# Queueing modulations behind the short convolution, casts of summed weights behind operand splits, and gate loads behind adding DMAs

## The chip, the core and the metric

The kernel runs on one core of one Trainium2 chip. The metric is device time in microseconds (us) for one launch. In the text PE is TensorE, DVE is VectorE, ACT is ScalarE, POOL is GpSimd and SP is SyncE; PEld is the load of stationary weights into PE. "L857" is line 857 of the kernel before. Every engine works through its own queue in order: an instruction that waits holds up all that stand behind it on the same engine.

## The reference

One layer of a hybrid encoder over 1024 tokens of 1024 channels, in fp32:

```
mod = silu(c) @ w_ada + b_ada                 # six vectors of 1024
h   = rms_norm(x) * (1 + sc1) + sh1
b_s, c_s, v_s, v_c, gl_c, gates = split(h @ w_in)      # w_in: 1024 x 7168
y_a = (b_s * causal_conv3(c_s * v_s)) @ w_short_out
u   = silu(layer_norm(causal_conv31(v_c * sigmoid(gl_c)) + bias))
y_b = u @ w_conf_out
x  += g1 * ((sigmoid(gate_a) * y_a + sigmoid(gate_b) * y_b) @ w_o)
h2  = rms_norm(x) * (1 + sc2) + sh2
x  += g2 * ((silu(h2 @ w_a) * (h2 @ w_b)) @ w_ffn_out)
out = rms_norm(x)
```

The vector `mod` depends on `c` alone, so its pieces can be computed at any time before they are used; g1, sc2, sh2 and g2 are wanted only after the projections and the mixers.

## The kernel before

**Matmuls.** All channels lie on partitions (128 at a time) and the 1024 tokens along the free axis, in two halves of 512. To keep fp32 accuracy each operand is split into a high part (a rounding cast, on ACT) and a low part (operand minus high part, on DVE or POOL); for weights that is `wh` (L243) and `wl` (L244). Each tile product is then three matmuls, high x high (L504), high x low (L505) and low x high (L507).

**Products and duals.** A matrix product is taken in 2 x 2 blocks with seven block products instead of eight; they are named "1265734" in the order in which they run. Products "5", "6", "7" and "3" need sums of weight blocks and of operand blocks. A *dual* is a pair of row blocks of the output that go through the seven products together. The input projection has 14 duals; duals 3 to 9 make the pairs u (conformer input), p (c_s * v_s) and q (b_s), duals 10 to 13 the gates. Results build up in PSUM banks "x", "y" and "z", and DVE and ACT read them out after each product (L866, L869, L873, L922). W_short_out (the "ya" stage), W_conf_out ("yb"), W_o and the two FFN matrices follow. In yb the two duals 0 and 1 are interleaved by `CONF_ORDER`: (0,"1") (1,"1") (0,"2") (1,"2") (0,"5") (1,"5") (0,"6") (1,"6") (0,"3") (0,"7") (1,"7") (0,"4") (1,"4") (1,"3").

**Weights.** They are fetched and split two products ahead. SP loads raw blocks (L227). In duals 3 to 9 POOL adds blocks and makes `wl`. In yb the sums are made in two ways: product "6" adds on DVE (L407), while "5", "7" and "3" use an adding DMA on POOL's queue (L397), which adds the second block to the raw tile that holds the first.

**Work between the products.** The depthwise convolution over 31 taps runs on DVE (L1158), one tap per instruction, spread over the input projection. The short convolution of a finished p row (`short_conv`: two ACT instructions at L854, then four DVE instructions at L857) uses the dual's two "x" banks as scratch; PE may write these banks again only when L857 is through. The pieces of `mod` are dot products of a 128 x 1024 block of w_ada with silu(c), one DVE instruction each (`modulation_of`, L485). Fourteen of these are spread over duals 3 to 9, two in each, at products "3" and "5" (`MOD_AT`). The block is loaded into the raw buffer that `dual_units.home` names, and the L485 is queued behind the product's last matmul.

**Order.** The program is traced once, and a scheduler at build time orders each engine's queue; `tc.issue_after(ins)` makes what is traced inside it stand behind `ins` in its queue. It adds no wait of its own. The order that comes out is static.

**Yb's side work.** The operands of each product are split as z..h (ACT, L544) and z..l (DVE, L545), the operands of "6" after a sum on DVE (t2z, L557). The results are multiplied by the gates: `gates_b` loads gate tiles `gb` on POOL's queue (L1421), DVE multiplies, and an adding DMA on POOL's queue (L1394) adds the product to the merged tile `ma`.

Of the kernel before, what the change touches and what calls it, by code (L numbers as in the profile page):

```python
# [38 lines left out]
ALU = mybir.AluOpType  # L39
# [28 lines left out]
BEGUN = 2  # L68
# [33 lines left out]
GATED = 10  # L102
# [17 lines left out]
CONF_ORDER = [(d, m) for m in "1256" for d in range(2)] + [(0, "3")] + [(d, m) for m in "74" for d in range(2)] + [(1, "3")]  # L120


MOD_FROM, MOD_AT = 16, "53"

# [12 lines left out]
def block_kernel(ctx: ExitStack, tc: tile.TileContext, x0, xT, c, vecs, ada, w_first, w_plain, w_duals,  # L139
                 w_short, w_conf, w_o, w_fi, w_fo0, w_fo1, outT):  # L140
    nc = tc.nc

    def pool(name, bufs, **kw):
        return ctx.enter_context(tc.tile_pool(name=name, bufs=bufs, **kw))
# [13 lines left out]
    rawp = pool("raw", 3)  # L158
# [8 lines left out]
    rawbp = pool("raw_b", 2, side="right")  # L167
# [7 lines left out]
    def hl_tile(name, dt=F32R):  # L175
        return tp.tile([P, H], dt, tag="t", name=name)
# [7 lines left out]
    def f32(t):  # L184
        return t.bitcast(F32)

    halves = (slice(0, H), slice(H, T))
# [21 lines left out]
    def col(base, k):  # L209
        return vec[:, base + k : base + k + 1]  # L210

    def modc(i):
        return mod[:, i : i + 1]
# [4 lines left out]
    def raw_tile(n=1024, home=None):  # L218

        if home is None:  # L220
            raws.append(raws.pop(0))
        return (home or raws[-1]).tile([P, 1024], F32, tag="raw", name="raw")[:, :n]

    def load(src, n=1024, home=None):
        raw = raw_tile(n, home)
        with tc.issue_after(x1_load[0]) if x1_load else ExitStack():
            load.ins = nc.sync.dma_start(raw, src).ins  # L227
        return raw
# [8 lines left out]
    def split_w(raw, n, after=(), lo_engine=nc.vector):  # L237
        wh = whp.tile([P, 1024], F32R, tag="wh", name="wh")[:, :n]
        wl = wlp.tile([P, 1024], F32R, tag="wl", name="wl")[:, :n]
        with ExitStack() as order:  # L240
            for ins in after:
                order.enter_context(tc.issue_after(ins))
            hi = nc.scalar.copy(wh, raw)  # L243
            lo = lo_engine.tensor_tensor(wl, raw, f32(wh), ALU.subtract)  # L244
        split_w.hi, split_w.lo = hi.ins, lo.ins
        if n == T and lo_engine is nc.gpsimd:
            pool_los.append((hi.ins, lo.ins))
        return wh, wl
# [130 lines left out]

        return {m: (lambda m=m: unit(m)) for m in PRODUCTS}  # L380

    conf_homes = [rawp, rawbp, rawp]

    def conf_units(mats, d):


        a = {}
        mat = dict(zip(("11", "12", "21", "22"), mats))

        def get(b, home=None):  # L390
            if home is None:
                conf_homes.append(conf_homes.pop(0))
                home = conf_homes[-1]
            return load(mat[b], home=home)

        def add(raw, b):
            nc.gpsimd.dma_start(raw, mat[b], accum_op=ALU.add)  # L397
            return raw

        def unit(m):  # L400
            if m == "5":
                raw = a["s1"] = add(get("22"), "21")
            elif m == "6":
                lo = split_w.lo
                raw = a["s2"] = get("11", (rawp, rawbp)[d])
                with tc.issue_after(lo):
                    nc.vector.tensor_tensor(raw, raw, a["s1"], ALU.add)  # L407
            elif m == "7":
                raw = add(get("21"), "11")
            elif m == "3":  # L410
                raw = add(a["s2"], "12")
            else:
                raw = get({"1": "11", "2": "12", "4": "22"}[m])
            return split_w(raw, 1024)

        return {m: (lambda m=m: unit(m)) for m in PRODUCTS}

    def gated_units(mats):
# [46 lines left out]
    def next_w(ahead=AHEAD):  # L465

        fetch(ahead + 1)
        return ready.pop(0)
# [14 lines left out]
    def modulation_of(i, raw):  # L483
        b = ADA_ORDER[i]
        nc.vector.tensor_tensor_reduce(  # L485
            out=raw, in0=raw, in1=cs, scale=1.0, scalar=col(V_ADA, b),
            op0=ALU.mult, op1=ALU.add, accum_out=modc(b),
        )
# [27 lines left out]
    def product(banks, m, t, evac=None, between=None, y_tile=ps2_tile, z_tile=ps_tile, onto="", by_k=False):  # L516


        w = next_w()
        b = {"1": "x", "6": "x", "7": "x", "4": "x", "2": "y", "5": "z", "3": "z"}[m]  # L520
        n = len(t)
        if by_k:
            for k in range(n):
                for p in range(2):
                    c0 = (p * n + k) * P
                    mm3([banks[b, p]], slice(c0, c0 + P), w, [t[k]], m not in onto and k == 0, k == n - 1, m in onto)
            for p in range(2):
                evac(p, m, banks[b, p])
            return
        for p in range(2):  # L530
            if (b, p) not in banks:
                banks[b, p] = {"x": ps_tile, "y": y_tile, "z": z_tile}[b](b)
            ps = banks[b, p]
            for k in range(n):
                c0 = (p * n + k) * P
                mm3([ps], slice(c0, c0 + P), w, [t[k]], m in "125" and m not in onto and k == 0, k == n - 1, m in "6734" + onto)
            if evac:
                evac(p, m, ps)
            if between and p == 0:
                between()  # L540
# [158 lines left out]
    gate_dram = {(b, j): dram.tile([P, T], F32, name=f"gate_{b}{j}") for b in "ab" for j in range(KC)}  # L699

    def uc_tile(name, n=T + CK - 1, dt=F32):
        return ucp.tile([P, T + CK - 1], dt, tag="uc", name=name)[:, :n]
# [147 lines left out]
    def short_conv(j, p, banks):  # L850

        sc[j] = uc_tile(f"sc{j}", T)
        for h, ps in enumerate(banks):
            nc.scalar.activation(ps, p[:, h * H : (h + 1) * H], AF.Copy, scale=col(V_SW, j))  # L854
        for h, ps in enumerate(banks):
            for s in range(1, SK):
                nc.vector.scalar_tensor_tensor(  # L857
                    out=ps if s < SK - 1 else sc[j][:, halves[h]], in0=p[:, h * H + s : (h + 1) * H + s],
                    scalar=col(V_SW + s * KC, j), in1=ps, op0=ALU.mult, op1=ALU.add,
                )  # L860


    reads = []
# [200 lines left out]
    def more_operands():  # L1064

        for p in range(2):
            nc.scalar.copy(win_banks[0]["x", p], m1[p])
        sums = t_split.ins
        for m, i, h in (("5", 0, 0), ("7", 0, 1), ("4", KH, 0)):
            for k in range(KH):  # L1070
                if m == "7" and k:
                    with tc.issue_after(sums):
                        nc.vector.tensor_tensor(x[k, 1], x[k + KH, 1], x[k, 1], ALU.subtract)
                th[m][k] = t_pair("t")
                t_split(x[k + i, h], *th[m][k])
        reads.append((0.0, t_split.ins))
# [4 lines left out]
    b = {}  # L1081
# [152 lines left out]
    n_mod = 0  # L1234
    for d, m in win_order:
        if (d, m) == (n_duals - 2, PRODUCTS[-2]):
            q_steps.pop(0)()
        if d + 1 >= GATED and d + 1 < n_duals:
            if m == PRODUCTS[-3]:
                win_evacs[d + 1].begin()  # L1240
            elif m == PRODUCTS[-1]:
                for p in range(2):
                    win_evacs[d + 1].bring(p)
        if d + 1 < BEGUN and m == PRODUCTS[-1]:
            for p in range(2):
                nc.scalar.copy(win_banks[d + 1]["x", p], m1[2 * (d + 1) + p])
        mod_raw = load(ada[MOD_FROM + n_mod], home=dual_units.home) if m in MOD_AT and BEGUN < d < GATED else None
        with tc.issue_after(mm3.ins) if (d, m) == (0, "6") else ExitStack():
            product(win_banks[d], m, th[m], win_evacs[d], onto="2")
        if (d, m) == win_order[0]:  # L1250
            more_operands()
            begin_gated("2", next_w(), streams[3:], 1)
        if (d, m) == (0, PRODUCTS[-1]):
            for h in range(2):
                tot.append(hl_tile(f"tot{h}", dt=F32))
                nc.gpsimd.memset(tot[h], 0.0)
        if win_order.index((d, m)) >= len(win_order) - 7:
            q_steps.pop(0)()
        if mod_raw is not None:
            with tc.issue_after(mm3.ins):  # L1260
                modulation_of(MOD_FROM + n_mod, mod_raw)
            n_mod += 1
    while late:
        late.pop(0)()
# [149 lines left out]
    gbs = {}  # L1414

    def gates_b(d, m):
        row, h = {"2": (0, 0), "7": (1, 1), "3": (0, 1), "4": (1, 0)}.get(m, (0, None))
        for i in range(2 * (h is not None)):
            j = 4 * d + 2 * i + row
            gbs[j, h] = g_tile("gb")  # L1420
            nc.gpsimd.dma_start(gbs[j, h], gate_dram["b", j][:, halves[h]])  # L1421

    yb_banks = [{} for _ in range(2)]
    for p in range(2):
# [353 lines left out]
    for g in range(FINAL):  # L1778
        n = 2 * GROUPS[g] * P
# [216 lines left out]
```

## Time and profile before

| what | value |
|---|---|
| median of 3 runs | 1468.63 us (1468.36 to 1471.03) |
| the profiled execution's own time | 1469.08 us |
| its span from the first to the last instruction | 1467.3 us |
| PE busy | 1436.7 us (98%), granted clock 0.99 |
| DVE busy | 1215.4 us (83%) |
| ACT busy | 652.4 us (44%) |
| POOL busy | 522.6 us (36%) |

The profiled execution is 0.45 us above the median, and 1.78 us above its span. A busy PE does not show how fast its clock ran, so the count of matmuls in a stretch of fixed length says more than the busy share. The stages by time: first operands to about 150 us, duals 2 to 13 to about 565, ya to 650, yb to 733, W_o to 790, the FFN to 1440.

### The profile page before, as it was taken

The numbers are of one execution on the slowest core, as the hardware profiler recorded it, in microseconds if no ns is written. First come the engines' busy times: TensorE is split into PE (matmuls) and PEld (weight loads), VectorE is DVE, ScalarE is ACT, GpSimd is POOL, SyncE is SP. The second block draws the span as 40 slices with busy tenths as digits, with TensorE's granted clock in tenths as the row PEclk, the third lists the DMA queues.
The fourth block names the chain that finished last, engine by engine and source line by source line (L and its number), as shares of the span: only waits on it lengthen the run. The fifth ranks groups of instructions, "written<-read, shape, count | busy, mean of one in ns | idle before, by whom it ended". The sixth has DMA issues, their size and how long they took to land.

```text
span 1467.3 us, 17736 instructions
## 1 busy us (share of the span) xinstructions
PE 1436.7 (98%) x6322; PEld 1177.6 (80%) x6322; DVE 1215.4 (83%) x1665; ACT 652.4 (44%) x955; POOL 522.6 (36%) x496
## 2 busy tenths in 40 slices
PE   9999999999989999997999999999999999999997
PEld 4888888777878888886788888888888888888887
DVE  7987999899989999987897799877776666866676
ACT  4873333333333446565535465444444443322235
POOL 0017776776676562012221001110111015663405
PEclk9999999999999999998999999999999999999999
DMA  9743133232335569768694536655554449996903
GB/s 354 274 153 99 59 125 105 101 115 101 125 106 181 165 205 323 218 201 184 165 332 163 172 115 217 218 176 174 173 183 144 150 143 350 390 371 194 356 1 115
DMA packets 95946, 275.04 MB, mean 187 GB/s; under 512 B 10945, under 2 KB 12993, under 8 KB 95858
## 3 DMA queue, kind: packets, MB, share of 16 engines
q1 hardware_dynamic: 46672, 148.92, 30.0%
q0 software_dynamic: 44000, 111.36, 25.1%
q10 hardware_dynamic: 5186, 13.64, 2.4%
q8 instruction: 49, 0.80, 0.2%
q14 instruction: 39, 0.32, 0.1%
HBM read 203.09 MB, written 67.63 MB: 185 GB/s over the span
## 4 chain that ended last, share of the span: by engine, by line
PE 84%; DVE 6%; POOL 4%; issue 2%; DMA 2%; ACT 0%; POOLq 0%; DVEq 0%; ACTq 0%
PE bank L504 10%; PE bank L505 10%; PE bank L507 10%; PE x L507 8%; PE x L505 8%; PE x L504 8%; PE z L507 4%; PE z L505 4%; PE z L504 4%; PE y L505 2%; PE y L504 2%; PE y L507 2%; PE mix L505 2%; PE mix L504 2%; PE mix L507 2%
## 5 line engine op out<-in xcount | busy, mean ns | idle before, releaser
L243 ACT CAST wh<-raw 128x1024 fp32r<-128x1024 f32 (+2 forms) x254 | 262.9, 1037 | 423.9 <-PE bank L505 139.0
L244 DVE TENSOR_TENSOR wl<-raw,wh 128x1024 fp32r<-128x1024 f32 (+2 forms) x176 | 212.4, 1208 | 52.9 <-ACT wh L243 51.1
L244 POOL TENSOR_TENSOR wl<-raw,wh 128x1024 fp32r<-128x1024 f32 x78 | 194.2, 2494 | 112.4 <-ACT wh L243 112.4
L1158 DVE SCALAR_TENSOR_TENSOR c<-diff,vec,c 128x512 f32<-128x512 f32 x232 | 164.3, 746 | 1.0
L1634 POOL DMA_DIRECT2D hid<-stage x70 | 37.4, 535 | 342.6 <-DVE stage L553 322.5
L504 PE MATMUL bank<-th,wh 128*128 128x512 f32 x336 | 132.5, 394 | 10.1 <-DVE sc L857 10.1
L507 PE MATMUL bank<-th,wl 128*128 128x512 f32 x336 | 132.0, 393 | 0.0
L505 PE MATMUL bank<-tl,wh 128*128 128x512 f32 x336 | 131.7, 392 | 0.0
L504 PEld LDWEIGHTS bank<-th,wh 128*128 128x128 f32 x336 | 63.9, 190 | 25.0 <-DVE sc L857 11.7
L505 PEld LDWEIGHTS bank<-tl,wh 128*128 128x128 f32 x336 | 63.9, 190 | 13.3
L507 PEld LDWEIGHTS bank<-th,wl 128*128 128x128 f32 x336 | 63.6, 189 | 13.4
L1158 DVE SCALAR_TENSOR_TENSOR c<-u,wsum,c 128x512 f32<-128x512 f32 x96 | 69.7, 746 | 0.6
L504 PE MATMUL x<-th,wh 128*128 128x512 f32 x176 | 68.5, 389 | 0.0
L505 PE MATMUL x<-tl,wh 128*128 128x512 f32 x176 | 68.5, 389 | 0.0
L507 PE MATMUL x<-th,wl 128*128 128x512 f32 x176 | 68.4, 390 | 0.0
L552 ACT CAST stage<-g 128x512 fp32r<-128x512 f32 x60 | 37.3, 621 | 58.9 <-DMA hid<-stage 37.7
L553 DVE TENSOR_TENSOR stage<-g,stage 128x512 fp32r<-128x512 f32 x60 | 41.2, 688 | 24.8 <-ACT stage L552 24.6
L1658 POOL DMA_DIRECT2D th<-hid x77 | 41.1, 534 | 51.8 <-PE x L507 28.0
L485 DVE CUSTOM_DVE_ANT_0 raw<-raw,cs,vec 128x1024 f32<-128x1024 f32 x24 | 42.7, 1783 | 11.8 <-DMA raw<-in_ada 11.0
L1658 POOL DMA_DIRECT2D tl<-hid x77 | 41.2, 535 | 19.0 <-DMA tl<-hid 3.2
L264 DVE TENSOR_TENSOR raw<-raw 128x1024 f32<-128x1024 f32 (+1 forms) x15 | 17.8, 1187 | 31.4 <-DMA raw<-in_w_fi 19.0
L504 PE MATMUL bank<-t2h,wh 128*128 128x512 f32 x112 | 43.6, 389 | 0.0
(830 smaller groups left out, 4156.6 us busy)
## 6 DMA issues: line engine op xcount, KB each, us to landing
hid<-stage POOLq DMA_DIRECT2D x70, 512.0 KB, 4.5
raw<-in_w_duals SPq DMA_DIRECT2D x65, 512.0 KB, 3.7
raw<-in_w_fi SPq DMA_DIRECT2D x54, 512.0 KB, 4.5
th<-hid POOLq DMA_DIRECT2D x77, 256.0 KB, 5.9
tl<-hid POOLq DMA_DIRECT2D x77, 256.0 KB, 5.9
ada<-in_ada SPq DMA_DIRECT2D x24, 512.0 KB, 5.5
raw<-in_ada SPq DMA_DIRECT2D x24, 512.0 KB, 4.3
raw<-in_w_fo SPq DMA_DIRECT2D x16, 512.0 KB, 6.1
```

Of the source, the lines that this page charges most:

```text
L243: hi = nc.scalar.copy(wh, raw)
L244: lo = lo_engine.tensor_tensor(wl, raw, f32(wh), ALU.subtract)
L264: eng.tensor_tensor(a["s1"], a["21"], a["22"], ALU.add)
L485: nc.vector.tensor_tensor_reduce(out=raw, in0=raw, in1=cs, scale=1.0, scalar=col(V_ADA, b), op0=ALU.mult, op1=ALU.add, accum_out=modc(b),)
L504: nc.tensor.matmul(ps, wh, xh, start=first, stop=False, skip_group_check=again)
L505: nc.tensor.matmul(ps, wh, xl, start=False, stop=False, skip_group_check=again)
L507: mm3.ins = nc.tensor.matmul(ps, wl, xh, start=False, stop=last, skip_group_check=again).ins
L552: t_split.act = nc.scalar.copy(hi, src).ins
L553: t_split.ins = nc.vector.tensor_tensor(lo, src, f32(hi), ALU.subtract).ins
L1158: tap.ins = nc.vector.scalar_tensor_tensor(out=out, in0=src[:, s : s + H], scalar=wt, in1=acc, op0=ALU.mult, op1=ALU.add).ins
L1634: nc.gpsimd.dma_start(hid_dram[key], s)
L1658: nc.gpsimd.dma_start(t, hid_dram[key][:, s])
```

## The change

There are three edits.

```diff
-MOD_FROM, MOD_AT = 16, "53"
+MOD_FROM = 16
...
-    conf_homes = [rawp, rawbp, rawp]
+    conf_homes, conf_adds = [rawp, rawbp, rawp], []
...
         def add(raw, b):
-            nc.gpsimd.dma_start(raw, mat[b], accum_op=ALU.add)
+            conf_adds.append(nc.gpsimd.dma_start(raw, mat[b], accum_op=ALU.add).ins)
             return raw
...
-            return split_w(raw, 1024)
+            return split_w(raw, 1024, () if m in "12" else (split.act, split.ins))
...
-                nc.vector.scalar_tensor_tensor(
+                short_conv.ins = nc.vector.scalar_tensor_tensor(
                     out=ps if s < SK - 1 else sc[j][:, halves[h]], in0=p[:, h * H + s : (h + 1) * H + s],
                     scalar=col(V_SW + s * KC, j), in1=ps, op0=ALU.mult, op1=ALU.add,
-                )
+                ).ins
...
-        mod_raw = load(ada[MOD_FROM + n_mod], home=dual_units.home) if m in MOD_AT and BEGUN < d < GATED else None
...
-        if mod_raw is not None:
-            with tc.issue_after(mm3.ins):
-                modulation_of(MOD_FROM + n_mod, mod_raw)
+        for n in range('55'.count(m) * (BEGUN < d < GATED)):
+            with tc.issue_after(short_conv.ins):
+                modulation_of(MOD_FROM + n_mod, load(ada[MOD_FROM + n_mod], home=(dual_units.home,dual_units.home)[n_mod % 2]))
             n_mod += 1
...
-            nc.gpsimd.dma_start(gbs[j, h], gate_dram["b", j][:, halves[h]])
+            with tc.issue_after(conf_adds[-1]) if conf_adds else ExitStack():
+                nc.gpsimd.dma_start(gbs[j, h], gate_dram["b", j][:, halves[h]])
```

**Edit A** issues both modulations of a dual at product "5" (before: one at "5", one at "3"), loads their blocks after the product instead of before it, and queues both L485 behind the last short-convolution instruction traced so far instead of behind the product's matmuls. On DVE, at dual 8, where two p rows are convolved (sc_3038 and sc_3045; p_2832 is the second row's input), the rows are these before:

```order
L485 ISA raw,mod<-raw,cs,vec 128x1024
L485 ISA mod 128x1
L1158 SCALAR_TENSOR_TENSOR c_4368<-diff,vec,c_4368 128x512 x2
L857 SCALAR_TENSOR_TENSOR bank<-p_2817,vec,bank 128x512 x2
L857 SCALAR_TENSOR_TENSOR sc_3038<-p_2817,vec,bank 128x512 x2
L869 TENSOR_TENSOR sc_3038<-bank,sc_3038 128x512
L857 SCALAR_TENSOR_TENSOR bank<-p_2832,vec,bank 128x512
L485 ISA raw,mod<-raw,cs,vec 128x1024
L485 ISA mod 128x1
L857 SCALAR_TENSOR_TENSOR sc_3045<-p_2832,vec,bank 128x512
```

and in the changed kernel these:

```order
L857 SCALAR_TENSOR_TENSOR bank<-p_2817,vec,bank 128x512 x2
L857 SCALAR_TENSOR_TENSOR sc_3038<-p_2817,vec,bank 128x512 x2
L869 TENSOR_TENSOR sc_3038<-bank,sc_3038 128x512
L857 SCALAR_TENSOR_TENSOR bank<-p_2832,vec,bank 128x512 x2
L857 SCALAR_TENSOR_TENSOR sc_3045<-p_2832,vec,bank 128x512 x2
L706 MEMSET u_3082 128x30
L485 ISA raw,mod<-raw,cs,vec 128x1024
L485 ISA mod 128x1
L485 ISA raw,mod<-raw,cs,vec 128x1024
L485 ISA mod 128x1
```

All eight L857 now stand ahead of both L485. The rows p_1001, p_1834, p_2094 and p_2328 change in the same way, with four L857 each.

**Edit B** queues the cast and the subtraction of every yb weight, except for products "1" and "2", behind the operand split (ACT and DVE) that was traced last. On ACT, around the operands z6 of product "6", the queue before reads

```order
L243 CAST wh<-raw 128x1024
L544 CAST z6h<-t2z 128x512
L1275 ACTIVATE cv_4987<-cv_4987,vec 128x512
L243 CAST wh<-raw 128x1024
L544 CAST z6h<-t2z 128x512
L1401 COPY vz<-y 128x512 x2
L544 CAST z6h<-t2z 128x512 x2
L1401 COPY vz<-bank 128x512 x2
L544 CAST z3h<-cv_4835 128x512
```

and in the changed kernel (whose lines 1274 and 1400 are the old 1275 and 1401)

```order
L544 CAST z6h<-t2z 128x512
L1274 ACTIVATE cv_4987<-cv_4987,vec 128x512
L544 CAST z6h<-t2z 128x512
L243 CAST wh<-raw 128x1024
L1400 COPY vz<-y 128x512 x2
L544 CAST z6h<-t2z 128x512 x2
L243 CAST wh<-raw 128x1024
L1400 COPY vz<-bank 128x512 x2
L544 CAST z3h<-cv_4835 128x512
```

Each of the two casts moves back: the cast for (1,"6"), which stood ahead of the first z6h, stands behind the second, and the cast for (0,"3"), which stood ahead of the second z6h, stands behind the fourth.

**Edit C** queues each gate load behind the last adding DMA of the weights traced so far. On POOL's queue, in the same place, before:

```order
L1394 DMA ma_4731<-gb 128x512
L1394 DMA ma_4745<-gb 128x512
L1421 DMA gb<-gate_b_121 128x512
L1421 DMA gb<-gate_b_123 128x512
L397 DMA raw<-in_w_conf 128x1024 x2
```

and in the changed kernel (L1393 is the old L1394):

```order
L1393 DMA ma_4731<-gb 128x512
L1393 DMA ma_4745<-gb 128x512
L397 DMA raw<-in_w_conf 128x1024 x2
L1421 DMA gb<-gate_b_119 128x512
L1421 DMA gb<-gate_b_121 128x512
```

The two adding DMAs, for (0,"3") and (0,"7"), stand directly behind the adds into `ma`, ahead of the gate loads 119, 121 and 123.

## The prediction

> **What bounds the kernel now.** I read the page first, then what PE waited for, then the stretches in which it waited.
>
> ```profile
> PE 1436.7 (98%) x6322; PEld 1177.6 (80%) x6322; DVE 1215.4 (83%) x1665; ACT 652.4 (44%) x955; POOL 522.6 (36%) x496
> ```
>
> PE is busy 98% of the span, so nothing can be won except where PE stands still or runs at a lowered clock. The list of PE's waits has only two entries of size:
>
> ```profile
> PE bank L504 <- DVE sc L857: 10.1, 4, 4.8
> PE bank L504 <- ACT z6h L544: 8.4, 1, 8.4
> PE clock L720 <- DVE ones_r L738: 1.6, 1, 1.6
> ```
>
> Four waits, 10.1 us together, are for the short convolution, and one of 8.4 us is for an operand split in yb. The third kind lies at the start, where nothing is changed. A wait also costs the matmuls that run slowly after it. For that I count matmuls in stretches of 10 us (columns: PE busy with its count, PEld, DVE, ACT, POOL, PE clock, DMA share, GB/s) against an undisturbed 100 us:
>
> ```profile
> 450.00:550.00 100.00, 100.00 (x443) 82.82 (x442) 97.05 (x128) 43.40 (x64) 62.84 (x30) 1.00 0.62 188
> 270.00:280.00 10.00, 8.26 (x36) 6.50 (x36) 10.00 (x16) 2.69 (x5) 2.82 (x2) 1.00 0.47 160
> 310.00:320.00 10.00, 8.26 (x37) 6.53 (x36) 9.64 (x16) 2.70 (x5) 2.92 (x2) 1.00 0.48 160
> 350.00:360.00 10.00, 8.22 (x29) 6.27 (x29) 9.89 (x17) 2.71 (x4) 3.07 (x2) 0.83 0.46 154
> 430.00:440.00 10.00, 5.21 (x18) 3.94 (x17) 9.92 (x14) 4.68 (x7) 5.48 (x2) 0.85 0.56 195
> 680.00:690.00 10.00, 3.22 (x15) 2.33 (x13) 2.54 (x4) 0.74 (x2) 4.42 (x6) 0.81 0.97 208
> 690.00:700.00 10.00, 8.41 (x27) 6.75 (x28) 8.45 (x13) 3.74 (x6) 0.00 (x0) 0.68 0.63 157
> 700.00:710.00 10.00, 9.76 (x41) 6.89 (x40) 6.23 (x9) 7.48 (x13) 0.00 (x0) 1.00 0.33 106
> ```
>
> 443 matmuls in 100 us are 44.3 in 10 us, or 0.226 us each. The four stretches of the duals lack 8.3, 7.3, 15.3 and 26.3, together 57.2 matmuls or 12.9 us. The three of yb hold 83 of 132.9 and lack 49.9, or 11.3 us. So at most 24.2 us are to be had, and the floor is 1469.08 - 24.2 = 1444.9 us by the profiled execution, 1444.4 by the median, which is 0.45 lower.
>
> **Edit A, what it removes.** At the first of the four waits DVE and ACT do this:
>
> ```profile
> 262.92 1.30 ACT L854 ACTIVATE bank<-p,vec 128x512 f32<-128x512 f32 x2
> 261.77 3.38 DVE L1158 SCALAR_TENSOR_TENSOR c<-diff,vec,c 128x512 f32<-128x512 f32 x5
> 268.92 2.60 DVE L485 CUSTOM_DVE_ANT_0 raw<-raw,cs,vec 128x1024 f32<-128x1024 f32 x1 [3.77 <-DMA raw<-in_ada]
> 272.10 1.40 DVE L857 SCALAR_TENSOR_TENSOR bank<-p,vec,bank 128x512 f32<-128x512 f32 x2
> 273.42 1.40 DVE L857 SCALAR_TENSOR_TENSOR sc<-p,vec,bank 128x512 f32<-128x512 f32 x2
> ```
>
> L857 has its inputs at 264.2, when L854 ends, and DVE is free at 265.15. But the L485 ahead of it waits 3.77 us for its block of w_ada and works 2.60 us, so L857 starts at 272.10, 6.9 us late, and PE (waiting 1.7 us by the stretch 270 to 280) gets its banks. With L485 behind L857, some 5 us of margin take the place of this wait. The largest wait, at the dual with two p rows, is on the chain of waits (start, length):
>
> ```profile
> 422.98 3.57 DMA raw<-in_ada
> 426.71 1.29 DVE raw L485
> 433.35 3.28 DVE raw L485
> 436.64 0.67 DVE sc L857
> 437.36 0.79 PE bank L504
> ```
>
> Both L485 stand ahead of the last L857. Taken out they free DVE from 422.98 to 428.00 and from 433.35 to 436.64, 8.3 us, where PE lacks 26.3 matmuls (5.9 us). PE arrives earlier by what the first three waits free (30.9 matmuls, 7.0 us), so here L857's margin is 8.3 - 5.9 = 2.4 us plus what DVE has caught up by then, less 7.0.
>
> **Whether DVE can follow** is thus the question for A. It sums up as follows:
>
> ```profile
> L485 DVE CUSTOM_DVE_ANT_0 raw<-raw,cs,vec 128x1024 f32<-128x1024 f32 x10 | 21.5, 2155 | 8.9 <-DMA raw<-in_ada 8.9
> L431 DVE TENSOR_TENSOR raw<-raw 128x1024 f32<-128x1024 f32 x2 | 4.1, 2063 | 2.1 <-DMA raw<-in_w_duals 2.0
> L485 DVE CUSTOM_DVE_ANT_0 ada<-ada,cs,vec x24: 1276/1280/1284, 11.8 to 1058.2; 128x1024 f32<-128x1024 f32 x24
> 433.20 2.35 POOL L244 TENSOR_TENSOR wl<-raw,wh 128x1024 fp32r<-128x1024 f32 x1 [7.89 <-ACT wh L243]
> ```
>
> From 270 to 480 DVE idles 8.9 us for w_ada and 2.0 for weights; both can go, since behind L857 the loads have 5 us more. Also, ten L485 take 2155 ns where one alone takes 1280, together 8.75 us: the one at 433.35 ends 1.0 us after POOL's L244 ends. I expect the L485 to meet POOL as often as now and book none of this. DVE then wins 10.9 us by 480 (bounds 8.9 and 8.9 + 2.0 + 8.75 = 19.6) and PE 12.9, so DVE falls 2.0 us further behind PE (bounds 4.0 and none). Seven duals hold their DVE work unchanged. What DVE can be behind shows where it is furthest, at dual 11:
>
> ```profile
> 507.95 0.68 DVE L866 TENSOR_TENSOR sig<-bank,sig 128x512 f32<-128x512 f32 x1
> 509.62 0.39 PE L504 MATMUL bank<-th,wh 128*128 128x512 f32 x1
> ```
>
> The read-out of product "7" ends at 508.63 and PE writes the same bank for "4" at 509.62: 1.0 us to spare. 2.0 - 1.0 = 1.0 us of waiting is left, so **A gives 12.9 - 1.0 = 11.9 us** (bounds 12.9 and 12.9 - 3.0 = 9.9). The margin at the two-p dual is 2.4 + 5.2 (8.9 less the 3.7 from 422.98 to 426.71 counted there already) - 7.0 = 0.6 us, thin but positive.
>
> [...]
>
> **Edits B and C.** The chain of waits through yb:
>
> ```profile
> 674.81 7.18 DMA ma<-gb
> 682.28 0.55 POOL gb L1421
> 682.83 7.04 DMA raw<-in_w_conf
> 689.97 1.04 ACT wh L243
> 691.01 0.53 ACT z6h L544
> 691.59 1.22 PE bank L504 x2
> ```
>
> The second z6h stands on ACT behind the cast for (0,"3"). That cast waits for its adding DMA, which stands on POOL behind gate loads that wait for the buffers of the adds into ma. C issues the adding DMA when its raw tile is free, some 5 us sooner (about 677.8), so it lands near 677.8 + 7.04 = 684.9. B moves the cast behind the fourth z6h, so z6h no longer depends on either. What is late next is DVE, which stood still here:
>
> ```profile
> 677.12 1.22 DVE L407 TENSOR_TENSOR raw<-raw 128x1024 f32<-128x1024 f32 x1
> 679.50 1.23 DVE L244 TENSOR_TENSOR wl<-raw,wh 128x1024 fp32r<-128x1024 f32 x1
> 691.04 1.23 DVE L244 TENSOR_TENSOR wl<-raw,wh 128x1024 fp32r<-128x1024 f32 x1 [8.51 <-ACT wh L243]
> ```
>
> Laid out in the new order from 677.12 with the lengths that these instructions have now (0.60 us from start to start for a 128 x 512 row, 1.14 for L244 and L407), DVE gives z6l of the four operands at 680.7, 683.1, 686.7 and 689.1, with one L244 between the second and the third. PE starts product "6" at 681.2 and interleaves four groups, so it wants the third z6l after 25 matmuls (686.9) and the fourth after 36 (689.4): on time by 0.2. PE then ends "6" at 692.1, and the first z3h, behind the read-out of (0,"6") on ACT, is ready at about 692.5 and z3l at 693.1, so about 1.0 us of waiting stays. **B and C give 11.3 - 1.0 = 10.3 us** (upper bound 11.3; lower bound 6, if DVE comes 4 us later here, the length of the two L407 and L244 ahead of z6, and again 1.0 is left). The adding DMA shares the DMA engines with the gate loads (0.97 busy in 680 to 690); even 4 us later, at 689, it would land as the cast's turn comes.
>
> All that follows yb has no PE wait in the list, so it moves up unchanged, and so does the 1.78 us of the profiled time outside its span. No instruction is added.
>
> **Sum.** 1469.08 - 11.9 - 10.3 = 1446.9 us by the profiled execution, less 0.45: **1446.4 us** for the median.
>
> **Rivals.**
>
> *A's waits only move.* Two L485 in a row each meet a POOL instruction: 2.35 + 1.28 = 3.6 us instead of 2.155, 1.5 us more for each of 14, or 21 us of DVE time; DVE then wins nothing by 480 and PE waits at L866 or L857 for all that A was to free. For it: DVE is 97% busy from 450 to 550. Against: between the pairs POOL idles too (7.89 us ahead of 433.20). Only B and C remain: 1468.63 - 10.3 = 1458.3 us. Half of it gives 1452.
>
> *Yb's wait only moves.* The weights for (1,"6") or (0,"3") now come too late, or the fourth z6l does, and PE loses the 11 us in smaller pieces. For it: margins of 0.2 us. Against: the cause of the 8.51 us in which DVE stood is gone. Only A remains: 1456.7 us.
>
> *Slower.* On SP the weight loads of the next dual stand behind the loads of w_ada:
>
> ```profile
> 264.50 7.38 SPq L227 DMA_DIRECT2D raw<-in_ada  x2
> 271.96 6.29 SPq L227 DMA_DIRECT2D raw<-in_w_duals  x4
> 280.93 2.41 POOL L244 TENSOR_TENSOR wl<-raw,wh 128x1024 fp32r<-128x1024 f32 x1 [5.09 <-ACT wh L243]
> ```
>
> The raw buffers come free when L485 has read them, and both L485 now come later. If that delays four blocks per dual by more than POOL's slack of 5.09 us, PE waits for weights in each of seven duals. It decides from 5.09 + 22.2 / 7 = 8.3 us of delay; at 10 us the loss is 7 x 4.9 = 34 and the time 1446.4 + 34 = 1480. Against: only 2.8 us of L857 move ahead of the L485 (the two rows from 272.10), while 3.77 us of idle time ahead of the first go.
>
> **How the numbers follow.** The forecast (A above 9, B and C above 6) has 0.62, the first rival with its half 0.18, the second 0.13, the slower one 0.03; 0.04 stay for both waits only moving, no change. The forecast's own range is 1444.4 to 1452.7 (A 9.9, B and C 6). With the first two rivals, 1443.8 to 1459 leaves out less than 0.2. About 0.2% (2.9 us) is what a measurement here can tell from no change: faster 0.93, same 0.04, slower 0.03.
>
> **What would show it.** In the list of PE's waits the entry for L857 is gone or under 1 us, that for z6h too; a new one of about 1 us for L866 near dual 11, and one for z3h or z3l. The L485 show no idle time for in_ada above 3 us; their mean stays near 2155 ns (above 3000 means the first rival). The stretches that held 36, 37, 29 and 18 matmuls hold 43 to 45. POOL's L397 pair is issued before 680 less the shift of 12 us. An entry of PE for wl or wh in duals 3 to 9 would prove the slower rival; a sum of PE waits above 8 us would make the prediction wrong.

## The result and the profile after

The changed kernel takes 1449.53 us (median of four runs, 1449.05 to 1451.0) against 1468.49 us for the kernel before on the same chip, a ratio of 0.987 with a 95% interval of 0.9853 to 0.9887. It is 19 us faster; 22.2 us were forecast. The profiled execution took 1449.05 us, 20.0 us less than the one before.

PE's waits in the changed kernel:

```profile
PE bank L504 <- DVE sig L866: 3.7, 1, 3.7
PE clock L720 <- DVE ones_r L738: 1.6, 1, 1.6
PE bank L504 <- DVE sc L869: 0.3, 1, 0.3
PE clock L720 <- DVE newton L779: 0.3, 1, 0.3
```

The four waits on L857 and the one on z6h are gone. What has come in their place is one wait of 3.7 us, and it lies in the duals. The stretches of 10 us show the same (columns as in the prediction):

```profile
270.00:280.00 10.00, 10.00 (x46) 8.29 (x45) 10.00 (x17) 3.66 (x5) 4.56 (x2) 1.00 0.64 210
310.00:320.00 10.00, 10.00 (x46) 8.26 (x44) 10.00 (x16) 3.03 (x5) 6.40 (x3) 1.00 0.58 205
350.00:360.00 10.00, 10.00 (x46) 8.29 (x45) 9.93 (x16) 3.18 (x4) 7.01 (x4) 1.00 0.42 137
430.00:440.00 10.00, 10.00 (x46) 8.29 (x45) 8.96 (x13) 3.96 (x6) 6.80 (x3) 1.00 0.43 127
460.00:470.00 10.00, 7.89 (x35) 6.09 (x33) 9.93 (x13) 5.23 (x7) 7.15 (x3) 1.00 0.22 64
470.00:480.00 10.00, 8.40 (x30) 6.79 (x31) 10.00 (x17) 1.78 (x3) 4.26 (x4) 0.83 0.61 155
680.00:690.00 10.00, 10.00 (x45) 8.01 (x44) 8.86 (x14) 8.72 (x17) 0.89 (x1) 1.00 0.77 230
690.00:700.00 10.00, 10.00 (x46) 8.29 (x45) 10.00 (x15) 3.60 (x6) 2.92 (x4) 1.00 0.85 193
```

The stretches that lacked matmuls now hold 45 or 46. Of those shown only 460 to 480 lacks some: 65 of 92, or 27 x 0.226 = 6.1 us, since the clock fell to 0.83 behind the wait.

DVE at the first of the four places shows edit A at work. L857 comes first, then both L485 back to back, without idle time and at 1.28 us:

```profile
266.00 1.41 DVE L857 SCALAR_TENSOR_TENSOR bank<-p,vec,bank 128x512 f32<-128x512 f32 x2
267.31 1.41 DVE L857 SCALAR_TENSOR_TENSOR sc<-p,vec,bank 128x512 f32<-128x512 f32 x2
269.24 1.28 DVE L485 CUSTOM_DVE_ANT_0 raw<-raw,cs,vec 128x1024 f32<-128x1024 f32 x1
270.45 1.28 DVE L485 CUSTOM_DVE_ANT_0 raw<-raw,cs,vec 128x1024 f32<-128x1024 f32 x1
```

L857 starts at 266.00 and not at 272.10. Where the new wait comes from is told by DVE and POOL some 28 us before it:

```profile
442.52 7.97 DVE L1150 TENSOR_TENSOR diff<-u 128x526 f32<-128x526 f32 x1
```

```profile
442.36 2.73 POOL L244 TENSOR_TENSOR wl<-raw,wh 128x1024 fp32r<-128x1024 f32 x1
444.72 2.86 POOL L1189 TENSOR_TENSOR tot<-tot,u 128x512 f32<-128x512 f32 x2
447.21 2.71 POOL L244 TENSOR_TENSOR wl<-raw,wh 128x1024 fp32r<-128x1024 f32 x1
```

L1150 prepares the seventh convolution: a subtraction with two inputs. In the kernel before the same instruction takes 0.69 us:

```profile
454.96 0.69 DVE L1150 TENSOR_TENSOR diff<-u 128x526 f32<-128x526 f32 x1
```

Here it takes 7.97 us and ends 0.6 us after the last of four POOL instructions that follow one another without a pause. From there to the wait on L866 at 471, in dual 10, DVE has no idle time in which to make this up (it is busy for 20.30 of the 20.37 us from 450.50 to 470.87).

In yb the cast for (0,"3") no longer stands ahead of the second z6h (ACT of the changed kernel, from the second z6h on; the cast at 673.01 is the one for (1,"6")):

```profile
672.48 0.62 ACT L544 CAST z6h<-t2z 128x512 fp32r<-128x512 f32 x1 [0.99 <-DVE t2z L557]
673.01 1.04 ACT L243 CAST wh<-raw 128x1024 fp32r<-128x1024 f32 x1
678.96 1.05 ACT L243 CAST wh<-raw 128x1024 fp32r<-128x1024 f32 x1
682.25 2.19 ACT L544 CAST z3h<-cv 128x512 fp32r<-128x512 f32 x4
```

The cast at 678.96, for (0,"3"), no longer waits for its adding DMA, and the first z3h is ready at about 682.9, before PE is through with its 48 matmuls of product "6" (begun at 672.2, 48 x 0.227 = 10.9, so 683.1). The first matmul that reads z3h starts at 683.36.

### The profile page after: what moved, and what is told of

Same layout as the page of the kernel before. It is cut to its first block, busy times and chain, and to the rows that moved or that the text cites. A ratio compares the mean times of both kernels' runs of the same rounds, so it can differ in the third digit from the quotient of the medians.

```text
span 1447.3 us, 17740 instructions
## 1 busy us (share of the span) xinstructions
PE 1432.0 (99%) x6322; PEld 1175.1 (81%) x6322; DVE 1215.1 (84%) x1665; ACT 650.7 (45%) x955; POOL 522.0 (36%) x496
## 4 chain that ended last, share of the span: by engine, by line
PE 94%; DVE 3%; POOL 1%; issue 0%; DMA 0%; ACT 0%; POOLq 0%; DVEq 0%; ACTq 0%
PE bank L505 13%; PE bank L504 13%; PE bank L507 13%; PE x L507 8%; PE x L504 8%; PE x L505 8%; PE z L507 4%; PE z L504 4%; PE z L505 4%; PE y L505 3%; PE y L507 3%; PE y L504 3%; PE mix L505 2%; PE mix L504 2%; PE mix L507 2%; PE lead L500 1%
## 5 line engine op out<-in xcount | busy, mean ns | idle before, releaser
L244 DVE TENSOR_TENSOR wl<-raw,wh 128x1024 fp32r<-128x1024 f32 (+2 forms) x176 | 212.3, 1207 | 37.6 <-ACT wh L243 35.6
L244 POOL TENSOR_TENSOR wl<-raw,wh 128x1024 fp32r<-128x1024 f32 x78 | 194.3, 2498 | 96.1 <-ACT wh L243 91.7
L507 PEld LDWEIGHTS bank<-th,wl 128*128 128x128 f32 x336 | 63.5, 189 | 13.2
L505 PEld LDWEIGHTS bank<-tl,wh 128*128 128x128 f32 x336 | 63.4, 189 | 13.2
L505 PE MATMUL bank<-t2l,wh 128*128 128x512 f32 x112 | 43.6, 389 | 0.0
```

Of the source, the lines that this page charges most:

```text
L505: nc.tensor.matmul(ps, wh, xl, start=False, stop=False, skip_group_check=again)
L507: mm3.ins = nc.tensor.matmul(ps, wl, xh, start=False, stop=last, skip_group_check=again).ins
```

## The experiments

The theory to be tested: the edits act in two separate stages and add; A works by the order of L485 and L857 on DVE; and what A did not bring was lost to L1150, which the new order laid onto POOL's unbroken run. The rivals stand with each run.

**Edit A alone.**

```diff
 # of the change only the edits to short_conv and the modulations
+        for n in range('55'.count(m) * (BEGUN < d < GATED)):
+            with tc.issue_after(short_conv.ins):
```

> Edit A alone. Theory (the edits act in separate stages and simply add; the block of L1150 by POOL follows from the two queues' order and not from chance): the four waits on L857 are gone, L1150 of the seventh convolution again takes 7 to 8 us, PE waits about 3.7 us on L866, and the time is 1468.5 - 7.5 = 1461 us (1459.5 to 1462). Rival (the long L1150 was an accident of one execution): L1150 takes at most 2.9 us, no PE wait above 1 us in the duals, 1468.5 - 13.5 = 1455 us.

Measured: 1462.0 us (1460.13 to 1462.02) against 1468.98, ratio 0.9951 (0.9937 to 0.9966): 7.0 us. PE's waits:

```profile
PE bank L504 <- ACT z6h L544: 8.8, 1, 8.8
PE bank L504 <- DVE sig L866: 3.8, 1, 3.8
```

Its L1150 takes this long, against POOL's run in the same place:

```profile
442.32 8.00 DVE L1150 TENSOR_TENSOR diff<-u 128x526 f32<-128x526 f32 x1
```

The time lies at the upper end of what was expected. The long L1150 is no accident of one execution; it comes with edit A.

**Edits B and C without A.**

```diff
+            return split_w(raw, 1024, () if m in "12" else (split.act, split.ins))
...
+            with tc.issue_after(conf_adds[-1]) if conf_adds else ExitStack():
```

> Edits B and C without A. Theory (adding): the 8.4 us wait on z6h is gone and no other takes its place, as in the changed kernel; the four waits on L857 stay at 10.1 us; time 1468.5 - 12 = 1456.5 us (1455.5 to 1457.5). Rival (yb only fits because A has brought DVE earlier or later into it): a wait of 1 us or more on a z operand stays, 1458.3 us or more.

Measured: 1456.73 us (1456.2 to 1457.33), ratio 0.9919 (0.9902 to 0.9935): 12.25 us. PE's only wait beside those at the start:

```profile
PE bank L504 <- DVE sc L857: 10.7, 4, 5.4
```

12.25 + 7.0 = 19.2 us, where both together brought 19.0. The edits add.

**Edit B alone**, the line with `split_w` of the diff above.

> Edit B alone: casts behind operand splits, the adding DMA still behind the gate loads (landing near 690). Theory (the order on ACT is the cause, the landing is early enough for its own product): most of the gain, 10 to 12 us, 1456.5 to 1458.5 us, with at most 1.5 us of waiting for the weights of (0,3). Rival (both edits are needed, since the weights of (0,3) land too late): PE waits 3 us or more at (0,3), 1462 us or more.

Measured: 1458.68 us (1457.69 to 1459.99), ratio 0.9932 (0.9918 to 0.9947): 10.3 us. Its waits in yb, and the cast for (0,"3"):

```profile
PE bank L504 <- ACT z3h L544: 1.2, 1, 1.2
PE bank L505 <- DVE z3l L545: 0.5, 1, 0.5
```

```profile
690.31 1.05 ACT L243 CAST wh<-raw 128x1024 fp32r<-128x1024 f32 x1 [3.02 <-DMA raw<-in_w_conf]
692.22 2.19 ACT L544 CAST z3h<-cv 128x512 fp32r<-128x512 f32 x4
```

Without C the adding DMA still lands near 690, the cast waits 3.02 us for it, and the z3h behind the cast are late by 1.2 us. With 0.5 us on z3l PE waits 1.7 us, where at most 1.5 were expected, and the time is 0.2 us above the expected range. So B is most of the gain, and C is worth 1458.68 - 1456.73 = 2.0 us on top of it.

**Edit C alone**, the lines of `conf_adds` and `gates_b`.

> Edit C alone: the adding DMA ahead of the gate loads, the cast still ahead of the second z6h. Theory: the adding DMA is issued about 5 us sooner and the wait on z6h falls from 8.4 to about 3.5 us; time 1468.5 - 5 = 1463.5 us (1462 to 1465). Rival (the landing is set by the load of the DMA engines, not by the issue): wait 7 us or more, 1467 to 1468.5 us. Second rival (the landing alone was the cause): wait under 1 us, 1457 us.

Measured: 1464.57 us (1463.12 to 1465.86), ratio 0.997 (0.996 to 0.9981): 4.4 us. PE's wait on z6h, and the cast ahead of it on ACT:

```profile
PE bank L504 <- ACT z6h L544: 5.0, 1, 5.0
```

```profile
686.49 1.04 ACT L243 CAST wh<-raw 128x1024 fp32r<-128x1024 f32 x1 [5.84 <-DMA raw<-in_w_conf]
```

The adding DMA was issued 5.4 us sooner (POOL's L397 at 677.43, in the kernel before at 682.83), but the cast starts only 3.5 us sooner, at 686.5 and not at 690.0, so 5.0 us of waiting stay and not the expected 3.5. The wait falls by 3.4 us, about as much as the cast is earlier; taking the cast out of the way, as edit B does, removes the whole wait on z6h.

**POOL's run broken up.** The changed kernel, with the two L1189 of the sixth convolution further back on POOL's queue: they now stand behind two more L244 and an L438, at 460.0 instead of 444.7. The store of that convolution's output (L1186, on ACT's queue) moves with them, from 440.0 to 455.6. DVE runs its instructions in the same order.

```diff
-        hi, lo = lo_at(conv_at(j + 1))
+        hi, lo = lo_at(conv_at(j + 1) + (0.4 if j == 5 else 0))
```

> The changed kernel, with the two L1189 (adds of the sixth convolution's output into tot) two POOL instructions later, so that POOL pauses while L1150 of the seventh convolution waits; DVE's queue is the same. Theory (POOL's unbroken run of two-input instructions kept L1150 out, and its 5 us made DVE late for PE at dual 10): L1150 takes under 3.5 us, the PE waits on L869 and L866 (0.3 and 3.7 us) are gone or under 1 us, and with the slow clock behind them the time falls by 5 to 6.6 us to 1443 to 1444.5 us. Rival (DVE has no room left anyway and is only late somewhere else): PE waits of 2 us or more on L866 or L857 stay, 1447 to 1449.5 us.

Measured: 1443.44 us (1443.1 to 1444.5), ratio 0.9827 (0.981 to 0.9843), 6.1 us less than the changed kernel. PE's waits, and DVE and POOL at the place:

```profile
PE clock L720 <- DVE ones_r L738: 1.6, 1, 1.6
PE clock L720 <- DVE newton L779: 0.7, 1, 0.7
PE bank L504 <- DVE sig L866: 0.3, 1, 0.3
```

```profile
442.15 3.16 DVE L1150 TENSOR_TENSOR diff<-u 128x526 f32<-128x526 f32 x1
```

```profile
442.00 2.74 POOL L244 TENSOR_TENSOR wl<-raw,wh 128x1024 fp32r<-128x1024 f32 x1
446.39 2.40 POOL L244 TENSOR_TENSOR wl<-raw,wh 128x1024 fp32r<-128x1024 f32 x1 [1.65 <-ACT wh L243]
```

POOL now has nothing to do at 444.74, L1150 gets through at 445.31, and the wait of 3.7 us is gone. From the end of L1150 to the read-out that PE waited for, DVE takes 20.4 us in both versions (450.49 to 470.87, here 445.31 to 465.67), so the 5.2 us by which L1150 ends sooner all arrive at the read-out. That is the cause of what A fell short by. The 6.1 us won are the 6.1 us of matmuls that 460 to 480 lacked: waiting, and the clock of 0.83 behind it. This version beats both kernels.

**The control**: the same line on the kernel before.

> Control: the kernel before with only the two L1189 moved two POOL instructions later. Theory (the long L1150 came with edit A, which moved DVE's L1150 onto POOL's unbroken run): nothing to win here, L1150 under 3 us as before, 1468.5 us within 1.5 (1467 to 1470). Rival (the move of L1189 is a gain of its own, whatever A does): 1462 to 1466 us.

Measured: 1468.55 us (1467.23 to 1469.78) against 1468.08, ratio 1.0 (0.999 to 1.001). Moving L1189 is worth nothing of its own. Its L1150 take at most 2.894 us, as before. The 6.1 us were A's, and the store that moves along is worth nothing either.

**Edit A's queue without its loads.** From the kernel before: modulations at "5" and "3", loads ahead of the product, but L485 behind L857.

```diff
         if mod_raw is not None:
-            with tc.issue_after(mm3.ins):
+            with tc.issue_after(short_conv.ins):
```

> From the kernel before, one half of edit A: the modulations stay at products 5 and 3 with loads ahead of the product, but each L485 is queued behind the last L857 traced so far. Theory (what counts is the order of L485 and L857 on DVE): the four waits on L857 go, as with edit A, 1459 to 1462 us. Rival (the loads of w_ada and the buffers they hold must move too): L485 at product 5 still waits for its block and is passed on to later work; PE waits of 4 us or more, 1464 to 1468 us.

Measured: 1461.83 us (1460.43 to 1464.87), ratio 0.9952 (0.9937 to 0.9967). PE's wait in the duals:

```profile
PE bank L504 <- DVE sig L866: 3.7, 1, 3.7
```

The same as edit A in full (1462.0), down to the wait on L866.

**Edit A's loads without its queue.** The line changed against edit A alone:

```diff
         for n in range('55'.count(m) * (BEGUN < d < GATED)):
-            with tc.issue_after(short_conv.ins):
+            with tc.issue_after(mm3.ins):
```

> From the kernel before, the other half of edit A: both modulations at product 5 with loads behind it, but the L485 queued behind the product's last matmul as before. Theory (order on DVE decides): L485 stand ahead of L857 or between them wherever the matmul ends earlier, the waits on L857 stay or grow to 10 to 18 us, 1468 to 1478 us. Rival (the loads decide): waits on L857 fall under 4 us, 1460 to 1464 us.

Measured: 1468.74 us (1466.45 to 1470.32), ratio 0.9997 (0.9988 to 1.0006). Nothing is gained. The waits on L857, and DVE at the first of the four places:

```profile
PE bank L504 <- DVE sc L857: 10.0, 4, 4.7
```

```profile
269.15 1.70 DVE L485 CUSTOM_DVE_ANT_0 raw<-raw,cs,vec 128x1024 f32<-128x1024 f32 x1 [4.66 <-DMA raw<-in_ada]
271.44 1.40 DVE L857 SCALAR_TENSOR_TENSOR bank<-p,vec,bank 128x512 f32<-128x512 f32 x2
```

One L485 still stands ahead of L857 and still waits for its block, 4.66 us. The order on DVE is the whole gain of edit A; its loads and the move from "3" to "5" are not needed.

**More work for DVE.** The version with L1189 moved, plus a tap that is run four times instead of once (2.0 us of DVE work near 457 us; the value is the same).

```diff
-            tap(eo[:, :H, 1] if s == CK // 2 - 1 else a1, e, s, ...)
+            for _ in range(4 if (j, s) == (6, 0) else 1):
+                tap(eo[:, :H, 1] if s == CK // 2 - 1 else a1, e, s, ...)
```

> The changed kernel with the two L1189 moved, plus three superfluous taps (the first tap of the second half of the seventh convolution is run four times, 0.66 us each, 2.0 us of DVE work near 457 us that changes no value). Theory (DVE has no room left in duals 10 and 11: the wait of 0.3 us on L866 is its last reserve): PE waits of 1.2 to 2.3 us on L866 in duals 10 to 12, and 1444.8 to 1447 us. Rival (DVE still has 2 us to spare, the 0.3 us is an accident): PE waits under 0.6 us, 1443 to 1444.2 us.

Measured: 1443.55 us (1443.13 to 1443.79) against 1468.08, ratio 0.9828 (0.9813 to 0.9842). No time is lost and the 0.3 us on L866 are gone, so the theory missed here. The first read-out of product "7" in dual 11, without and with the extra taps:

```profile
493.82 0.68 DVE L866 TENSOR_TENSOR sig<-bank,sig 128x512 f32<-128x512 f32 x1
```

```profile
493.46 0.67 DVE L866 TENSOR_TENSOR sig<-bank,sig 128x512 f32<-128x512 f32 x1
```

With 2.0 us more to do, DVE comes to this read-out 0.36 us sooner. The scheduler has laid the queue anew. Between L1150 and this read-out stand 48 taps in both versions, so with the three extra ones ahead of it, three of the ordinary taps now come after it; and the L1149 ahead of it takes 0.69 us instead of 1.59. So the run doesn't measure how much room DVE has in a fixed order; it shows that the order changed with the amount of work, and that 2.0 us more of it cost PE nothing here.

## Why the prediction was right or wrong

**Direction and stages: right, and the mechanism but for one step of A.** The time lies inside the range. The four waits on L857 and the one on z6h went for the reasons that were given: the order of L485 on DVE (the two halves of A show it), the order of the cast on ACT (B alone: 10.3 us), the landing of the adding DMA as a smaller part (C: 2.0 us on top of B). No first matmul waited for weights in duals 3 to 9, so the slower rival did not come. All waits of PE in the list come to 5.9 us, under the 8 us that were named as the limit.

**A: 7.0 us where 11.9 were forecast, below its lower bound of 9.9.** The step that failed is "DVE then wins 10.9 us by 480". It shows at the first read-out of product "7" in dual 10, behind which PE writes the same bank for "4". In the kernel before:

```profile
478.87 0.68 DVE L866 TENSOR_TENSOR sig<-bank,sig 128x512 f32<-128x512 f32 x1
482.43 0.39 PE L504 MATMUL bank<-th,wh 128*128 128x512 f32 x1
```

In the changed kernel:

```profile
470.87 0.68 DVE L866 TENSOR_TENSOR sig<-bank,sig 128x512 f32<-128x512 f32 x1
471.60 0.68 PE L504 MATMUL bank<-th,wh 128*128 128x512 f32 x1 [3.71 <-DVE sig L866]
```

And with L1189 moved:

```profile
465.67 0.68 DVE L866 TENSOR_TENSOR sig<-bank,sig 128x512 f32<-128x512 f32 x1
```

PE wanted the bank at 467.89 (471.60 - 3.71), 14.5 us sooner than before. DVE came 8.0 us sooner, and before it had 2.9 us to spare (482.43 - 479.55). 14.5 - 8.0 - 2.9 = 3.6 us, about the wait of 3.7. With L1189 moved DVE comes 13.2 us sooner, and nothing waits here. The forecast had looked for the lag in dual 11, where the kernel before had only 1.0 us to spare, and not in dual 10.

From the first L857 (160.25 us before, 159.21 after) to this read-out DVE runs the same instructions, in 7.0 us less: 6.3 us less idle time and 0.6 us less busy time. "Seven duals hold their DVE work unchanged" thus holds for the sum, but not for the single instructions. The groups on DVE between 262 and 480 us, before and then after:

```profile
L1150 DVE TENSOR_TENSOR diff<-u 128x526 f32<-128x526 f32 x4 | 6.6, 1647 | 0.0
L1149 DVE TENSOR_TENSOR diff<-u 128x527 f32<-128x527 f32 x4 | 4.9, 1222 | 0.0
```

```profile
L485 DVE CUSTOM_DVE_ANT_0 raw<-raw,cs,vec 128x1024 f32<-128x1024 f32 x10 | 14.6, 1489 | 2.3 <-DMA raw<-in_ada 2.3
L1150 DVE TENSOR_TENSOR diff<-u 128x526 f32<-128x526 f32 x4 | 13.3, 3324 | 0.0
L1149 DVE TENSOR_TENSOR diff<-u 128x527 f32<-128x527 f32 x4 | 7.8, 1939 | 0.0
```

L485 lost less to POOL than "as often as now": 6.9 us won (21.5 - 14.6), of which nothing was booked. L431 and L432 won another 2.8 us (8.8 - 6.0). But L1149 and L1150 lost 9.6 us (21.1 - 11.5), and 7.3 (7.97 - 0.69) of it sit in the one L1150 at 442, behind which DVE was late for PE. Collisions with POOL did not go away when DVE's order changed; they moved to other instructions, and one of them took a large part at once.

The idle time, too, fell by less than the 10.9 us that were booked: by 6.6 ahead of L485 and by 0.2 ahead of L431 and L432. That was not what PE waited for: with L1189 moved DVE is idle no less in this stretch (9.5 us, 9.1 in the changed kernel), and all that PE waits for in the duals is 0.3 us.

The first rival named the right resource and the wrong victim. It expected the paired L485 to be held up, at a mean above 3000 ns; their mean fell to 1489. It was half realised (A at 59% of its forecast) by another instruction. With that collision removed A would be worth 7.0 + 6.1 = 13.1 us (an estimate from the two runs), and the left-over wait on L866 that was forecast at about 1.0 us for dual 11 is there, at 0.3 us.

L1150 ends 0.57 us after a POOL instruction in both versions: with L1189 moved, after the one L244 that it met (445.31 and 444.74); in the changed kernel, after the last of four in a row (450.49 and 449.92).

**B and C: 12.25 us where 10.3 were forecast, above the upper bound of 11.3.** Two terms were mis-sized. The 1.0 us of waiting that was to stay for z3h did not come: z3h was ready at about 682.9 and PE came to it no sooner than 683.1. And the count of lacking matmuls was made against 44.3 in 10 us, a tenth of the count in 100 us. A stretch of 10 us counts every matmul that touches it, and undisturbed it holds 46, as the rows of the changed kernel show. Against 46, yb lacked 138 - 83 = 55 matmuls or 12.4 us, and the four stretches of the duals 184 - 120 = 64 or 14.5 us. The floor was thus nearer to 1469.08 - 26.9 - 0.45 = 1441.7 than to 1444.4; the version at 1443.4 lies below the floor that the prediction gave.

**The sum** came within 3.1 us because the two errors have opposite signs: A 4.9 too high, B and C 2.0 too low, which leaves 2.9.

## What to carry to other kernels

An instruction that waits for a load belongs behind whatever another engine is waiting for; where it stands in its own queue can be worth all of the gain, and when its load is issued none of it (here 1461.83 us with the order alone and 1468.74 us with the loads alone, from 1469.04). Before booking freed time on an engine, look at what its later instructions will now lie beside: where two engines hold each other up, as DVE and POOL do here (in the changed kernel L1150 takes 7.97 us instead of 0.69, and POOL's L244 at 465.21, which starts while L432 runs, 3.39 us where the median from 262 to 480 is 2.41), the collision can pass to other instructions. A single one can be held longer (7.3 us here) than any of the waits on L857 that were removed (4.8 us at most), so look for it ahead of the places where another engine waits, and not only in the sum. To count lost matmuls, compare a stretch with undisturbed stretches of the same length.

## What was not expected of the hardware

A two-input subtraction on DVE of 0.69 us was held for 7.97 us (8.00 in the run with A alone), through four POOL instructions in a row, and got through 0.6 us after the last one. With a pause of 1.65 us behind the first of them it took 3.16 us. In other places DVE got its turn after one POOL instruction: L432 at 463.95 in the changed kernel took 2.39 us and ended 1.1 us after the L438 that it met (462.85 to 465.26), with an L244 right behind that L438. Why L1150 did not get in so was not settled.

The clock fell to 0.83 in the stretch 470 to 480, behind the wait of 3.7 us: the first matmuls start 0.43 us apart up to 475.06, the later ones 0.23. In the kernel before, the wait of about 1.8 us in the stretch 350 to 360 came with 0.83 too, while the two of 1.7 us (270 to 280 and 310 to 320) came with 1.00. What tells these apart no run shows.
